# Gated linear attention on one core: the decay of a chunk in pairs of levels with shared keys, in blocks of 32 tokens

## The chip, the cores and the metric

The kernel runs on one core of a Trainium2 chip. The metric is the device time of one execution in microseconds (us); the time given for a kernel is the median of several runs. The profile is that of one further execution.

## What is computed

Two residual layers over 512 tokens of width 1024: a sparse attention layer and a layer of gated linear attention (GLA), each followed by a squared-ReLU MLP. The change lies in the GLA mixer. It has 4 heads with keys of 128 and values of 256. Its reference, in chunks of tokens, cut to what matters:

```python
def step(state, inp):
    qi, ki, vi, gi = inp
    b = jnp.cumsum(gi, axis=2)
    diff = jnp.where(mask, b[:, :, :, None, :] - b[:, :, None, :, :], -jnp.inf)
    attn = jnp.einsum('bhid,bhjd,bhijd->bhij', qi, ki, jnp.exp(diff))
    intra = jnp.einsum('bhij,bhje->bhie', attn, vi)
    inter = jnp.einsum('bhid,bhde->bhie', qi * jnp.exp(b), state)
    ...
```

The part that matters is `attn`: for each pair of a query i and an earlier key j of the same chunk, the sum over the 128 key dimensions d of q[i,d] k[j,d] exp(b[i,d] - b[j,d]), where b is the running sum of log gates. The exponent depends on i, j and d, so it is no plain matrix product.

## The kernel before, in words

The kernel takes 512 tokens as 4 chunks of 128. Large products (the projections and the MLP) are done in three float32r matmuls on a high and a low part of each operand (`mm3`, lines 186 to 188); these are called main products below. Weights come in by SyncE's DMA queue as `raw`; ScalarE makes the high part (line 130) and VectorE the low part (line 131). PSUM tiles of the pool `qk` have two buffers.

In `gla`, `qT`, `kT` and `bT` (trace: gq, gk, gb) hold queries, keys and running gate sums with the key dimension on partitions, heads and tokens along the row. `AT[c]` is the transposed `attn` of chunk c: 128 keys on partitions, 4 heads x 128 queries. It is made level by level (`LEVELS` 64, 32, 16, 8, 4, 2, 1). At level H the chunk is cut in blocks of 2H tokens. For a query in the right half and a key in the left half of a block, the exponent is split at the left half's last token m: exp(b[i]-b[m]) on the query and exp(b[m]-b[j]) on the key. Each pair i > j lies in just one level; the pairs i = j are the diagonal (li = -1), plain q times k.

`prepare(c, li)` makes the factors of a level in a tile E (5 buffers): two subtractions of 256 columns on GpSimd (923, 924), one exponential of 512 on ScalarE (925), and two products with keys and queries on VectorE (926, 927). `apply(c, li)` multiplies: for levels 64 and 32 in tiles of 64 or 32 columns, written by ScalarE into AT (944, 945); for levels 16 to 1 in one whole 128 x 128 product per head (948), most of whose result is of no use, from which VectorE copies what a mask admits into AT (949, 128 x 512). The diagonal is a whole product too (935), times the identity (936).

`work` lists the 32 steps (c, li). `around(n, tile_work)` emits the preparation of the next n steps, then a tile of main products of a panel, then the application of these steps: 2 per tile in the first value panel (346 columns), 3 in the second and in the first gate panel (512 columns). The tile framework's scheduler then sets the order on each engine. In the last gate panel `chunk_in` and `chunk_out` finish the chunks: they multiply AT with the values (985), take the running state in (987), norm and gate, and update the state (1003). `constants` loads the masks during the MLP before.

Of the kernel before, what the change touches and what calls it, by code (L numbers as in the profile page):

```python
# [47 lines left out]
LEVELS = [64, 32, 16, 8, 4, 2, 1]  # L48
BLOCK = 32
N_MASKS = sum(h < BLOCK for h in LEVELS)  # L50
# [16 lines left out]
def _consts():  # L67
# [18 lines left out]
    cu = np.stack([((p // (2 * h)) == (f // (2 * h))) & (p % (2 * h) < h) & (f % (2 * h) >= h) for h in LEVELS if h < BLOCK], axis=1)  # L86
# [8 lines left out]
class Trunk:  # L95
# [752 lines left out]
    def gla(self, w3, ba, gn, masks):  # L848
# [3 lines left out]
        with tc.tile_pool(name="gla", bufs=1) as gp, tc.tile_pool(name="glt", bufs=2) as gt:  # L852
# [50 lines left out]
            AT = [gp.tile([P, B_H, P], F32, name=f"AT{c}") for c in range(NT)]  # L903

# [5 lines left out]

            work = [(c, li) for c in range(NT) for li in range(-1, len(LEVELS))]
            ready = {}

            def prepare(c, li):

                if li < 0:
                    return
                H, cs = LEVELS[li], slice(c * P, (c + 1) * P)
                b, q, k = bT[:, :, cs], qT[:, :, cs], kT[:, :, cs]
                E = gt.tile([P, B_H, P], F32, name="E", bufs=5)  # L920
                left, right = halves(b, 0, H), halves(b, 1, H)
                bm = left[:, :, :, H - 1:H].to_broadcast([P, B_H, P // (2 * H), H])
                nc.gpsimd.tensor_tensor(halves(E, 0, H), bm, left, op=OP.subtract)
                nc.gpsimd.tensor_tensor(halves(E, 1, H), right, bm, op=OP.subtract)
                nc.scalar.activation(E, E, AF.Exp, scale=IT)
                nc.vector.tensor_mul(halves(E, 0, H), halves(E, 0, H), halves(k, 0, H))
                nc.vector.tensor_mul(halves(E, 1, H), halves(E, 1, H), halves(q, 1, H))
                ready[c, li] = E

            def apply(c, li):  # L930
                cs = slice(c * P, (c + 1) * P)
                ps = self.qk.tile([P, 512], F32, name="qk").rearrange("p (h s) -> p h s", s=P)
                if li < 0:
                    for h in range(B_H):
                        nc.tensor.matmul(ps[:, h, :], kT[:, h, cs], qT[:, h, cs], start=True, stop=True)
                    nc.vector.tensor_tensor(AT[c], ps, self.ident[:, None, :].to_broadcast([P, B_H, P]), op=OP.mult)
                    return
                E = ready.pop((c, li))
                H = LEVELS[li]
                if H >= BLOCK:  # L940
                    for j in range(0, P, 2 * H):
                        left, right = slice(j, j + H), slice(j + H, j + 2 * H)
                        for h in range(B_H):
                            nc.tensor.matmul(ps[left, h, right], E[:, h, left], E[:, h, right], start=True, stop=True)
                        nc.scalar.copy(AT[c][left, :, right], ps[left, :, right])
                    return
                for h in range(B_H):
                    nc.tensor.matmul(ps[:, h, :], E[:, h, :], E[:, h, :], start=True, stop=True)  # L948
                nc.vector.copy_predicated(AT[c], masks[:, li - len(LEVELS) + N_MASKS, None, :].to_broadcast([P, B_H, P]), ps)

            def chunk_in(c):
# [3 lines left out]
                eb = gt.tile([P, B_H, P], F32, name="E", bufs=5)  # L955
# [16 lines left out]
            def chunk_out(c, last):  # L972
# [7 lines left out]
                for a in range(0, B_H, 2):  # L980
# [8 lines left out]
                    for j in range(2):  # L989
                        h = a + j  # L990
                        nc.scalar.activation(junk[:, :B_DV], o[:, j, :], AF.Square, accum_out=ss[:, h:h + 1])
# [178 lines left out]
```

## Time and profile before

| | |
|---|---|
| median of 3 runs | 1160.45 us (1160.43 to 1160.72) |
| the profiled execution's own time | 1162.37 us |
| its span, first to last instruction | 1160.6 us |
| mean granted TensorE clock | 0.996 |
| busy: TensorE, VectorE, ScalarE, GpSimd | 1144.4, 890.5, 556.9, 212.3 us |
| the steps of `work`, first to last product | about 648 to 731 us of the span |

The names of the profile: PE is TensorE (PEld its weight loads), DVE VectorE, ACT ScalarE, POOL GpSimd, SP SyncE, whose queue starts the DMAs. L948 is line 948 of the kernel. A matmul's record is longer than the time until the next one starts, since matmuls are pipelined; a busy share of PE therefore can't be read as work at full rate.

### The profile page before, as it was taken

The numbers are of one execution on the slowest core, as the hardware profiler recorded it, in microseconds if no ns is written. First come the engines' busy times: TensorE is split into PE (matmuls) and PEld (weight loads), VectorE is DVE, ScalarE is ACT, GpSimd is POOL, SyncE is SP. The second block draws the span as 40 slices with busy tenths as digits, with TensorE's granted clock in tenths as the row PEclk, the third lists the DMA queues.
The fourth block names the chain that finished last, engine by engine and source line by source line (L and its number), as shares of the span: only waits on it lengthen the run. The fifth ranks groups of instructions, "written<-read, shape, count | busy, mean of one in ns | idle before, by whom it ended". The sixth has DMA issues, their size and how long they took to land. (4 is left out here: it accounts for less than half of the span.)

```text
span 1160.6 us, 15685 instructions
## 1 busy us (share of the span) xinstructions
PE 1144.4 (99%) x5847; PEld 963.0 (83%) x5847; DVE 890.5 (77%) x1587; ACT 556.9 (48%) x953; POOL 212.3 (18%) x144
## 2 busy tenths in 40 slices
PE   8999999999999999999999999999999999999997
PEld 7877888888888888888888998888988888888875
DVE  6799997687886786687864577766697866886787
ACT  6665786544444353344355444343453534444342
POOL 0000000002213203212302254110032032213221
PEclk9999999999999999999999999999999999999998
DMA  7322130521431441242241231233223422431421
GB/s 245 100 73 73 37 110 1 160 87 37 145 106 42 143 140 62 90 145 86 74 133 50 64 112 35 70 109 110 74 60 122 145 70 76 145 107 46 138 73 73
DMA packets 58196, 109.35 MB, mean 94 GB/s; under 512 B 5204, under 2 KB 10712, under 8 KB 58120
## 3 DMA queue, kind: packets, MB, share of 16 engines
q1 hardware_dynamic: 56968, 104.16, 28.1%
q0 software_dynamic: 1152, 4.19, 1.3%
q8 instruction: 46, 0.75, 0.3%
q14 instruction: 30, 0.25, 0.1%
HBM read 106.24 MB, written 2.10 MB: 93 GB/s over the span
## 5 line engine op out<-in xcount | busy, mean ns | idle before, releaser
L131 DVE TENSOR_TENSOR w_lo<-raw,w_hi 128x1024 fp32r<-128x1024 f32 (+4 forms) x220 | 289.3, 1333 | 27.5 <-ACT w_hi L130 25.1
L130 ACT CAST w_hi<-raw 128x1024 fp32r<-128x1024 f32 (+4 forms) x220 | 223.4, 1024 | 121.4 <-PE ps L188 43.8
L186 PE MATMUL ps<-XT,w_hi 128*128 128x512 f32 (+1 forms) x640 | 236.1, 369 | 0.0
L187 PE MATMUL ps<-XT,w_hi 128*128 128x512 f32 (+1 forms) x640 | 235.7, 368 | 0.0
L188 PE MATMUL ps<-XT,w_lo 128*128 128x512 f32 (+1 forms) x640 | 235.6, 368 | 0.0
L186 PE MATMUL ps<-w_hi,XT 128*128 128x512 f32 (+5 forms) x440 | 164.5, 374 | 0.8 <-ACT w_hi L130 0.8
L187 PE MATMUL ps<-w_lo,XT 128*128 128x512 f32 (+5 forms) x440 | 161.8, 368 | 1.1 <-DVE w_lo L131 1.1
L188 PE MATMUL ps<-w_hi,XT 128*128 128x512 f32 (+5 forms) x440 | 161.6, 368 | 0.0
L186 PEld LDWEIGHTS ps<-XT,w_hi 128*128 128x128 f32 x640 | 120.7, 189 | 20.2 <-issue 0.2
L187 PEld LDWEIGHTS ps<-XT,w_hi 128*128 128x128 f32 x640 | 120.7, 189 | 20.2 <-issue 0.4
L188 PEld LDWEIGHTS ps<-XT,w_lo 128*128 128x128 f32 x640 | 120.7, 189 | 20.1 <-issue 0.2
L152 POOL TENSOR_TENSOR raw<-raw 128x1024 f32<-128x1024 f32 x14 | 34.2, 2440 | 385.4 <-DVE w_lo L131 385.4
L186 PE MATMUL ps<-w_hi,form 128*128 128x512 f32 x260 | 102.3, 393 | 0.7 <-DVE big L408 0.7
L187 PE MATMUL ps<-w_lo,form 128*128 128x512 f32 x260 | 101.5, 390 | 0.0
L188 PE MATMUL ps<-w_hi,form 128*128 128x512 f32 x260 | 101.4, 390 | 0.0
L187 PEld LDWEIGHTS ps<-w_lo,XT 128*128 128x128 f32 x440 | 83.5, 190 | 11.9 <-DVE w_lo L131 1.7
L186 PEld LDWEIGHTS ps<-w_hi,XT 128*128 128x128 f32 x440 | 83.5, 190 | 11.5 <-ACT w_hi L130 1.0
L188 PEld LDWEIGHTS ps<-w_hi,XT 128*128 128x128 f32 x440 | 83.5, 190 | 10.8
L131 DVE TENSOR_TENSOR w_lo<-t,w_hi 128x1024 fp32r<-128x1024 f32 x14 | 30.4, 2168 | 72.7 <-ACT w_hi L130 72.7
L360 DVE TENSOR_TENSOR h<-h 128x512 f32<-128x512 f32 (+1 forms) x72 | 43.7, 624 | 44.1 <-ACT h L359 44.1
L359 ACT ACTIVATE h<-ps 128x512 f32<-128x512 f32 (+1 forms) x72 | 38.7, 546 | 61.7 <-PE ps L188 54.7
L130 ACT CAST w_hi<-t 128x1024 fp32r<-128x1024 f32 x14 | 14.7, 1051 | 105.2 <-POOL t L154 105.2
(238 smaller groups left out, 1986.1 us busy)
## 6 DMA issues: line engine op xcount, KB each, us to landing
raw<-in_mlp_w_up_dram SPq DMA_DIRECT2D x64, 512.0 KB, 4.5
raw<-in_mlp_w_down_dram SPq DMA_DIRECT2D x64, 512.0 KB, 4.6
raw<-in_b_w_in_dram SPq DMA_DIRECT2D x16, 512.0 KB, 4.6
raw<-in_a_w_in_dram SPq DMA_DIRECT2D x12, 512.0 KB, 4.3
big<-in_x_dram SPq DMA_DIRECT2D x8, 512.0 KB, 4.1
raw<-in_a_w_o_dram SPq DMA_DIRECT2D x8, 512.0 KB, 4.0
raw<-in_b_w_o_dram SPq DMA_DIRECT2D x8, 512.0 KB, 5.0
raw<-in_b_w_in_dram SPq DMA_DIRECT2D x8, 346.0 KB, 4.3
```

What stands on the lines that cost most here:

```text
L130: self.nc.scalar.copy(hi, src)
L131: self.nc.vector.tensor_sub(lo, src, hi.bitcast(F32))
L152: sub(t1, b12, b11)
L186: mmul(out, lhs[0], rhs[0], start=first, stop=False, skip_group_check=more)
L187: mmul(out, lhs[0], rhs[1], start=False, stop=False, skip_group_check=more)
L188: mmul(out, lhs[1], rhs[0], start=False, stop=last, skip_group_check=more)
L359: nc.scalar.activation(h, ps[:, :step], AF.Relu)
L360: nc.vector.tensor_mul(h, h, h)
```

## The change

The levels 16 to 1 and the diagonal, six steps per chunk, become three: `None` (level 1 and the diagonal), (2, 4) and (8, 16). Such a step works in blocks of 32 tokens, and its pairs i > j lie within one block of 32, so its product is done per head and block: 4 products per head of 32 keys by 48 columns, each written to its own strip of 32 partitions of a PSUM tile.

For a pair (H, G) with G = 2H, the keys are scaled once, to the last token of their own run of H tokens (one subtraction and exponential of 512 columns, one product with all keys). A tile Q (2 buffers) holds three kinds of queries, 64 per head each: of the right halves at level H; of the right halves at level G, for keys of the nearer run; and these times the decay over one run, for keys of the farther one. The step `None` uses plain keys, and Q holds all queries (put in an order of even and odd by ScalarE) and the odd ones with their decay.

The results of a chunk gather in a tile `near`, 128 keys by 4 x 32 queries. VectorE multiplies the diagonal's part with a small identity `eye` into it and copies 16 columns per head through a mask, once for level 1 and three times for each pair. After the step (2, 4), ScalarE puts the four blocks of 32 x 32 per head to their places in AT, which GpSimd clears ahead of all steps. Levels 64 and 32 are done as before. E has 3 buffers instead of 5. `work` has 20 steps, whose levels 64 and 32 stand among the others; the tiles of the panels take 1, 2 and 2 steps. The table of masks shrinks from 640 to 144 columns. The gate's tanh is written to its final place without a tile of its own.

```diff
+            work = [(c, level) for c in range(NT) for level in WIDE]
+            for i in range(2 * NT):
+                work.insert(NT + 2 * i, (i // 2, (64, 32)[i % 2]))
+            def exps(E, *parts):
+                for e, x, y in parts:
...
+                    nc.gpsimd.tensor_tensor(e, x, y, op=OP.subtract)
+                nc.scalar.activation(E, E, AF.Exp, scale=IT)
+            def queries(c, level):
...
+                Q = gt.tile([P, B_H, 192], F32, name="Q")
...
+                exps(Q[:, :, :P], (e[0], halves(b, 1, H), near[:, :, :, H - 1:H]),
+                     (e[1], halves(b, 1, G), far[:, :, :, G - 1:G]))
+                nc.vector.tensor_mul(e[1], e[1], halves(q, 1, G))
...
+                nc.vector.tensor_mul(e[2], e[1], over.to_broadcast(list(e[2].shape)))
+                nc.vector.tensor_mul(e[0], e[0], halves(q, 1, H))
...
-                E = gt.tile([P, B_H, P], F32, name="E", bufs=5)
+                E = gt.tile([P, B_H, P], F32, name="E", bufs=3)
+                if isinstance(level, tuple):
+                    bs, es = (x.rearrange("p h (n s) -> p h n s", s=level[0]) for x in (b, E))
+                    exps(E, (es, bs[:, :, :, level[0] - 1:level[0]], bs))
+                    nc.vector.tensor_mul(E, E, k)
...
-                for h in range(B_H):
-                    nc.tensor.matmul(ps[:, h, :], E[:, h, :], E[:, h, :], start=True, stop=True)
-                nc.vector.copy_predicated(AT[c], masks[:, li - len(LEVELS) + N_MASKS, None, :].to_broadcast([P, B_H, P]), ps)
...
                 for h in range(B_H):
+                    for j in range(0, P, BLOCK):
+                        own = Q[:, h, :].rearrange("p (a m) -> p a m", a=3)[:, :, j // 2:(j + BLOCK) // 2]
+                        nc.tensor.matmul(ps[j:j + BLOCK, h, :48].rearrange("p (a m) -> p a m", a=3),
+                                         K[:, h, j:j + BLOCK], own, start=True, stop=True)
...
+                for s, m, o in parts:
+                    mk = masks[:, None, m * 16:(m + 1) * 16].to_broadcast([P, B_H, 16])
+                    nc.vector.copy_predicated(halves(near[c], 1, s), mk.rearrange("p h (n s) -> p h n s", s=s),
+                                              ps[:, :, o:o + 16].rearrange("p h (n s) -> p h n s", s=s))
+                if level == WIDE[-1]:
+                    for j in range(0, P, BLOCK):
+                        own = slice(j, j + BLOCK)
+                        nc.scalar.copy(AT[c][own, :, own], near[c][own])
...
-            for c0, steps in ((332, 2), (678, 3)):
+            for c0, steps in ((332, 1), (678, 2)):
...
-                    around(3, gate_tile)
+                    around(2, gate_tile)
```

The order on the engines. Outside the GLA mixer it is the same but for the line numbers. On TensorE, a place at which tiles of level 32 stand, in the value panels; before:

```order
L188 MATMUL ps<-w_hi,XT 128x346
L944 MATMUL qk<-E 32x32 x4
L948 MATMUL qk<-E 128x128 x2
L944 MATMUL qk<-E 32x32 x4
L948 MATMUL qk<-E 128x128 x2
L186 MATMUL ps<-w_hi,XT 128x346
```

And such a place of the change (L197 to L199 are the main products, L990 levels 64 and 32, L997 the small products):

```order
L199 MATMUL ps<-w_hi,XT 128x346
L990 MATMUL qk<-E 32x32 x4
L997 MATMUL qk<-Q,E 32x48 x12
L990 MATMUL qk<-E 32x32 x4
L997 MATMUL qk<-Q,E 32x48 x4
L197 MATMUL ps<-w_hi,XT 128x346
```

Between the two halves of level 32 twelve small products now stand, in other places 14 or 15, where two whole ones stood.

On TensorE, the place where the last gate panel begins; before:

```order
L188 MATMUL ps<-w_hi,XT 128x512
L948 MATMUL qk<-E 128x128 x8
L968 MATMUL tps<-cft,E 128x128 x4
L186 MATMUL ps<-w_hi,XT 128x512
L187 MATMUL ps<-w_lo,XT 128x512
L948 MATMUL qk<-E 128x128 x4
L188 MATMUL ps<-w_hi,XT 128x512
```

And of the change (L1034 are the transposes of the line 968 before):

```order
L199 MATMUL ps<-w_hi,XT 128x512
L990 MATMUL qk<-E 32x32 x4
L997 MATMUL qk<-Q,E 32x48 x15
L990 MATMUL qk<-E 32x32 x4
L997 MATMUL qk<-Q,E 32x48
L1034 MATMUL tps<-cft,E 128x128 x4
L197 MATMUL ps<-w_hi,XT 128x512
```

The last step's products no longer stand among the last panel's main products.

On GpSimd, the beginning of the stage in the change; L453 and L447 of the MLP before (here L464, L458) were followed by the subtractions at once:

```order
L464 TENSOR_TENSOR big<-big 128x512 x3
L916 MEMSET AT_6178 128x512
L916 MEMSET AT_6179 128x512
L916 MEMSET AT_6180 128x512
L916 MEMSET AT_6181 128x512
L935 TENSOR_TENSOR Q<-gb 128x4x64
L935 TENSOR_TENSOR E<-gb 128x512 x2
L935 TENSOR_TENSOR E<-gb 128x4x64 x2
L935 TENSOR_TENSOR Q<-gb 128x4x64 x5
```

Four clearings stand ahead of the first subtraction, and whole subtractions of 512 columns stand among the halves.

## Rows read from the trace of the kernel before

**Rows 1.** The page's first part: busy time of each engine.

```profile
PE 1144.4 (99%) x5847; PEld 963.0 (83%) x5847; DVE 890.5 (77%) x1587; ACT 556.9 (48%) x953; POOL 212.3 (18%) x144
```

**Rows 2.** Windows: stretch, its length, busy us by engine, granted clock, DMA share, GB/s.

```profile
648.00:728.00 80.00, 78.87 (x554) 71.60 (x553) 56.50 (x88) 36.76 (x64) 37.26 (x50) 1.00 0.21 69
```

**Rows 3.** Groups by line and shape, 620 to 740 us: busy, mean ns | idle before.

```profile
L948 PE MATMUL qk<-E 128*128 128x128 f32 x160 | 21.3, 280 | 1.0 <-DVE AT L949 1.0
L935 PE MATMUL qk<-gq,gk 128*128 128x128 f32 x32 | 4.3, 278 | 0.0
L944 PE MATMUL qk<-E 128*32 128x32 f32 x64 | 3.5, 199 | 0.2 <-ACT AT L945 0.2
L944 PE MATMUL qk<-E 128*64 128x64 f32 x32 | 2.7, 228 | 0.0
```

**Rows 4.** Timeline of PE from 659.5: start us, length us, merged records.

```profile
659.50 0.32 PE L188 MATMUL ps<-w_hi,XT 128*128 128x346 f32 x1
659.66 1.95 PE L948 MATMUL qk<-E 128*128 128x128 f32 x16
```

**Rows 5.** Timeline of PE at 654.13, within a run of 32-column tiles.

```profile
653.95 0.35 PE L944 MATMUL qk<-E 128*32 128x32 f32 x6
```

**Rows 6.** Timeline of PE at 649.60, within a run of 64-column tiles.

```profile
649.43 0.34 PE L944 MATMUL qk<-E 128*64 128x64 f32 x3
```

**Rows 7.** Timeline of PE from 120.9, in the attention layer.

```profile
120.93 1.05 PE L724 MATMUL po<-vn,pT 128*128 128x65 f32 x8
```

**Rows 8.** Timeline of PE from 672.8, in and out of 32-column tiles.

```profile
672.90 0.32 PE L188 MATMUL ps<-w_hi,XT 128*128 128x346 f32 x1
673.15 0.44 PE L944 MATMUL qk<-E 128*32 128x32 f32 x8
673.52 0.43 PE L186 MATMUL ps<-w_hi,XT 128*128 128x346 f32 x1
673.79 0.32 PE L187 MATMUL ps<-w_lo,XT 128*128 128x346 f32 x1
```

**Rows 9.** Timeline of PE from 690.9; eight 64-column and eight 32-column records, merged.

```profile
691.00 0.32 PE L188 MATMUL ps<-w_hi,XT 128*128 128x346 f32 x1
691.25 1.05 PE L944 MATMUL qk<-E 128*64 128x64 f32 x16
692.22 0.50 PE L186 MATMUL ps<-w_hi,XT 128*128 128x512 f32 x1
```

**Rows 10.** Timeline of PE from 726.3, around the last whole products.

```profile
726.51 0.39 PE L187 MATMUL ps<-w_lo,XT 128*128 128x512 f32 x1
727.88 1.13 PE L948 MATMUL qk<-E 128*128 128x128 f32 x8 [0.97 <-DVE AT L949]
...
729.07 0.39 PE L186 MATMUL ps<-w_hi,XT 128*128 128x512 f32 x1
729.30 0.39 PE L187 MATMUL ps<-w_lo,XT 128*128 128x512 f32 x1
```

**Rows 11.** Groups of the other engines, 620 to 740 us.

```profile
L923 POOL TENSOR_TENSOR E<-gb 128x256 f32<-128x256 f32 x28 | 21.8, 779 | 111.9 <-DVE gb L891 62.7 <-PE qk L944 20.3 <-ACT big L1030 14.3
L924 POOL TENSOR_TENSOR E<-gb 128x256 f32<-128x256 f32 x28 | 20.3, 726 | 0.0
L925 ACT ACTIVATE E<-E 128x512 f32<-128x512 f32 x28 | 17.7, 632 | 30.8 <-POOL E L924 30.8
L949 DVE COPY_PREDICATED AT<-masks,qk 128x512 f32<-128x512 uint8 x20 | 14.7, 734 | 9.3 <-PE qk L948 5.9 <-ACT AT L945 3.4
L1042 POOL TENSOR_TENSOR gate<-gate,gn 128x512 f32<-128x512 f32 x5 | 6.6, 1320 | 14.2 <-DVE gate L1040 14.2
L936 DVE TENSOR_TENSOR AT<-qk,cft 128x512 f32<-128x512 f32 x4 | 2.7, 680 | 1.6 <-PE qk L935 1.6
L945 ACT COPY AT<-qk 32x128 f32<-32x128 f32 x8 | 2.0, 251 | 2.1 <-PE qk L944 2.1
```

More of the change, by code (lines that the diff above doesn't have):

```diff
@@ L47 @@
 TAU = 16.0
-LEVELS = [64, 32, 16, 8, 4, 2, 1]
+WIDE = (None, (8, 16), (2, 4))
 BLOCK = 32
-N_MASKS = sum(h < BLOCK for h in LEVELS)
+N_MASKS = 7
 NEG_MASKED = -3.0e38
@@ L85, in _consts, with mask @@
     cf = np.concatenate([a.astype(np.float32) for _, a in parts], axis=1)
-    cu = np.stack([((p // (2 * h)) == (f // (2 * h))) & (p % (2 * h) < h) & (f % (2 * h) >= h) for h in LEVELS if h < BLOCK], axis=1)
+    k, q = p % BLOCK, f[:, :BLOCK]
+    def mask(size, keys, half):
+        r = q[:, q[0] % size >= half]
+        return (k // size == r // size) & (k % size >= keys[0]) & (k % size < keys[1])
+    cu = [mask(2, (0, 1), 1)]
+    for h in (8, 2):
+        cu += [mask(2 * h, (0, h), h), mask(4 * h, (h, 2 * h), 2 * h), mask(4 * h, (0, h), 2 * h)]
+    cu = np.concatenate(cu + [k == q[:, 0::2], k == q[:, 1::2]], axis=1)
     return np.ascontiguousarray(cf), np.ascontiguousarray(cu.reshape(P, -1).astype(np.float32))
@@ L903, in gla @@
             AT = [gp.tile([P, B_H, P], F32, name=f"AT{c}") for c in range(NT)]
+            for a in AT:
+                nc.gpsimd.memset(a, 0.0)
             def halves(x, i, s):
                 return x.rearrange("p h (n two s) -> p h n two s", two=2, s=s)[:, :, :, i, :]
[L911 to L916, printed above, removed]
-                    return
-                H, cs = LEVELS[li], slice(c * P, (c + 1) * P)
-                b, q, k = bT[:, :, cs], qT[:, :, cs], kT[:, :, cs]
-                E = gt.tile([P, B_H, P], F32, name="E", bufs=5)
[L921 to L928, printed above, removed]
@@ L943, in apply @@
+            def apply(c, level):
+                K, Q = ready.pop((c, level))
+                if level in (64, 32):
+                    ps = self.qk.tile([P, 512], F32, name="qk").rearrange("p (h s) -> p h s", s=P)
+                    for j in range(0, P, 2 * level):
+                        left, right = slice(j, j + level), slice(j + level, j + 2 * level)
                         for h in range(B_H):
-                            nc.tensor.matmul(ps[left, h, right], E[:, h, left], E[:, h, right], start=True, stop=True)
+                            nc.tensor.matmul(ps[left, h, right], K[:, h, left], Q[:, h, right], start=True, stop=True)
@@ new lines, in apply @@
+                if level is None:
+                    near[c] = gt.tile([P, B_H, BLOCK], F32, name="near")
+                    nc.vector.tensor_tensor(near[c].rearrange("p h (m two) -> p h two m", two=2),
+                                            ps[:, :, :BLOCK].rearrange("p h (two m) -> p h two m", two=2),
+                                            eye[:, None, :, :].to_broadcast([P, B_H, 2, 16]), op=OP.mult)
+                    parts = [(1, 0, 32)]
+                else:
+                    m = 1 + 3 * (level == (2, 4))
+                    parts = [(level[0], m, 0), (level[1], m + 1, 16), (level[1], m + 2, 32)]
```

71 lines of the change are left out of this document (46 added, 25 removed).

## The prediction

> **What bounds the kernel now.** I read the busy shares first, then the stage by windows, then the groups of instructions, then the timeline of TensorE. PE is busy over 99% of the span [rows 1], which by itself says little, since records of a pipelined engine overlap. The stage that the change touches, from 648 to 728 us, shows the same: PE 78.9 of 80 us, DVE 56.5, ACT 36.8, POOL 37.3, at a granted clock of 1.00 (the 2.4 GHz level) [rows 2]. So what counts there is the spacing of PE's records and the few places at which PE waits; the other engines lie beside it. An fp32 matmul of the program leaves two records, so the 24 matmuls of a chunk at levels 16 to 1 and on the diagonal are 48 records, 192 over four chunks; the groups list 160 and 32 of them [rows 3].
>
> The spacing of records in a run is read from a merged row: its length, less the duration of one record, over the count less one. For 128 columns loaded and 128 streamed: (1.95 - 0.28)/15 = 0.111 us [rows 3, 4]. For tiles of 32 columns with 32 streamed: (0.35 - 0.199)/5 = 0.030 us inside a run [rows 3, 5], or (0.44 - 0.199)/7 = 0.034 us with the slower first step of a run [rows 3, 8]. For 64 and 64: (0.34 - 0.228)/2 = 0.056 us [rows 3, 6]. A row of the attention has 128 columns loaded and 65 streamed, and its records of about 0.275 us stand (1.05 - 0.275)/7 = 0.111 us apart [rows 7]: the larger of the two widths sets the spacing, at about 0.9 ns per column.
>
> **What PE loses.** The 96 whole products, 192 records x 0.111 = **21.3 us**, all on the path.
>
> **What PE gains.** Three steps for each of four chunks, each with 16 matmuls of 32 columns loaded and 48 streamed: 192 matmuls, 384 records. No row shows this shape. In width it lies between 0.030 (32) and 0.056 (64), which are 11.5 and 21.5 us; if nothing overlaps, half way between them, 0.043, or 16.5 us. What is new besides is that each matmul goes to the next strip of 32 output partitions, where the 32-wide tiles of before stay in one strip through a run. I take 0.034, the whole run of eight 32-column records [rows 8]: the weight load is the same, and of the 16 more columns streamed I expect that they lie beside the neighbour strip's load. 384 x 0.034 = **13.1 us**.
>
> **Going into and out of tiles.** From the main product at 672.90 to the second one after the tiles at 673.79 it is 0.89 us [rows 8]; two main products at 0.16 and eight records at 0.030 make 0.56, so an excursion costs 0.33: 0.09 before the first tile, 0.13 before the next main product starts, the rest behind it. The run with both tile sizes takes 1.22 us from 691.00 to 692.22 [rows 9]; less one main product, 8 x 0.056 and 8 x 0.030, and the 0.09 and 0.13, 0.15 is left for the change between the sizes. Before there are 11 excursions and 1 such change; in the changed order I count 12 and 4. That adds 0.33 + 3 x 0.15 = **0.8 us**.
>
> **PE's waits.** Before, PE loses 1.14 us at 726.51 (1.37 to the next record, less the 0.23 of one main product of 512 columns) ahead of a product that needs the buffer of the one before [rows 10], and 0.2 ahead of a second half of level 32 [rows 3]: 1.3 together. In the changed order all steps stand ahead of the last gate panel, so the first goes. The second half of level 32 still waits for ScalarE's copy of the first (0.25 us [rows 11]); 12 to 15 small products now stand between, 0.8 to 1.0 us. For new waits on the two qk buffers I charge half of what goes: **-0.7 us**, with 0 and -1.3 as ends.
>
> **Beside PE.** DVE sheds 20 masked copies of 0.734 and 4 diagonal products of 0.680, 17.4 us [rows 11], and gets 28 copies of 64 elements and 4 products of 128. Pro rata these are 3.2 us, at the price of the old ones 23.3; I estimate 0.25 each, 8 us, nearer the lower end, as an eighth of the elements is copied. Its products are 56 halves before, and now 40 halves and 8 whole ones, worth 56: even. ACT sheds 4 of 28 exponentials at 0.632 for half ones, and gets 4 query copies (taken as 0.63) and 16 placements of 32 partitions at 0.25: about +6 us on 36.8 of 80. POOL's 56 half subtractions, at 0.779 and 0.726 42 us, become 36 halves and 8 whole ones at 1.32 (the row of the same size), 38 us, plus 4 clearings of AT, under 1.32 each. Those stand ahead of its first subtraction, before which it waited 62.7 us [rows 11]. All of this fits beside PE and costs nothing; where that cover fails is the third rival. The smaller table, cast and mask load lie in the MLP before and change no wait of PE. SP's order is the same.
>
> **The sum.** -21.3 + 13.1 + 0.8 - 0.7 = -8.1 us. The execution profiled took 1162.37 us with a span of 1160.6; the sum makes it 1154.3. The median of the three runs stands 1.9 lower, at 1160.45, so the forecast is **1152.3 us**. After this stage PE stays busy up to the end, so what is saved is not given back.
>
> A rule of the Trainium skill speaks against the change. Row first: 32-column records stand 0.030 us apart and 64-column ones 0.056 [rows 5, 6], so the narrow ones pay half, and the trace does not bear the rule out. The Trainium skill, "TensorEngine Tiling (Array Packing)", section "Instruction Overhead", has it that a matmul pays some 60 cycles whatever it streams, and that one column is as slow as 60. By that, 48 columns would cost what 60 do.
>
> **Rivals.**
>
> *Serial strips.* Strips do not overlap at all and the larger width sets the spacing: 0.043 x 384 = 16.5, sum -4.7, **1155.8 us**. For it: every row above follows the larger width. Against: none of them changes strip inside a run. It gets 0.31.
>
> *Sixty columns.* The narrow records cost what 60 columns would, 60 x 0.9 = 0.053: 20.4 us, sum -0.8, **1159.7 us**, no change. The rows of 32 columns are against it. 0.03. (This is the rule just named.)
>
> *Strips side by side.* All four strips load and stream at once: 0.043/4 = 0.011, 4.1 us, sum -17.1, **1143.4 us**. No row shows fewer than 0.030 between any two records of this kind, and the two records of one matmul share a strip, so they can't overlap. 0.05. The Trainium skill's "TensorEngine Tiling (Array Packing)", section "Key Properties", says that tiles work independently and load and multiply in parallel; no run so far shows it here.
>
> *A wait in place of the products.* Key and query buffers: E has 3 instead of 5, Q 2, so POOL can prepare less far ahead. In a value tile with two steps it has one whole and four half subtractions, 1.32 + 4 x 0.75 = 4.3 us [rows 11]; PE has 24 x 0.16 + 32 x 0.034 + 8 x 0.030 + 0.33 + 0.15 = 5.6 us. It decides from 1.07 us per half on; at 1.5 us POOL is 1.7 us late in each of the four such tiles, and 6.9 us of the gain go: **1159.2 us**. The gate tiles stream 512 columns and have more cover. For it: POOL's halves vary where DVE works beside them (mean 0.779, where the other half has 0.726). Against: a whole tile of slack in the first panel. 0.09.
>
> *Each change of strip drains PE* (the other side). The size changes show 0.09 us each on the way in [rows 8]. If going to another strip of the same size costs the same, all 192 matmuls pay: 17.3 us on the serial case, +12.6, **1173.1 us**. It decides from 0.024 us per change on (4.7/192), measured from the serial case. No row excludes it, as no run of tiles in this trace changes strip. 0.08. By the Trainium skill, "TensorEngine Tiling (Array Packing)", section "Key Properties", it is a change of mode, and not of the tile alone, that drains the engine; the rows show the drain at changes of size and say nothing on the other.
>
> **How the numbers follow.** The forecast, records from 0.030 to 0.038 apart (1150.7 to 1153.9), has 0.44. The serial case has 0.31 and, with the ends of the waits, reaches 1155 to 1158. The range starts at 1147.5: two strips side by side, 0.022, give 8.3 us and -12.9. It ends at 1158.0. Left out are the four strips (0.05), the drain (0.08) and most of the late buffers and the sixty columns (some 0.08). A measurement of this kernel can tell 0.2%, 2.3 us: under 1158.1 is faster, over 1162.8 slower. Faster: 0.44 + 0.05 + 0.30 of the serial case = 0.79. Same: 0.01 of the serial case, 0.03 of the sixty columns, 0.07 of the late buffers = 0.11. Slower: the drain with 0.08 and 0.02 of the late buffers = 0.10.
>
> **What would show it.** In the group of the small products: 384 records, and the merged rows of 32 of them about 1.3 us long; 1.55 and more is the serial case, under 0.9 side by side, 3 or more the drain. The group of masked copies on DVE should be under 0.4 us each, and its idle time should grow. Ahead of the small products PE should show under 1 us of idle time in all; several us there, ended by DVE or by ACT's exponentials, would be the late buffers. Main products must keep their spacing of 0.16 and 0.23 us [rows 4, 10]. The forecast is wrong if the stage's gain on PE is under 6 or over 11 us, or if a gain there comes back as idle time of PE later.

## The result and the profile after

Four runs of the change give a median of **1145.52 us** (1145.34 to 1149.05), four of the kernel before 1160.59 (1160.43 to 1162.27): a ratio of **0.9874, 95% interval 0.9853 to 0.9895**. The gain is 15.1 us where 8.1 were forecast, and the time lies 2 us under the range. Runs of one kernel differ by 2 to 4 us, so where single times are compared below, they are those of its fastest runs: about 1160.2 for before, 1145.4 for the change. TensorE's clock has a part in this: in the profiled execution of before the granted clock is 0.83 from 20 to 30 us, which is 3.4 of the 10 us at half (1.2 GHz); in that of the change it is 1.00 there and through the stage.

The stage runs from the first small product to the first product of the chunks' output. The PE timelines of the kernel before and of the change show these two places (start us, length us, then the record):

```profile
648.28 1.06 PE L935 MATMUL qk<-gq,gk 128*128 128x128 f32 x8
...
733.86 1.02 PE L985 MATMUL po<-big,AT 128*128 128x256 f32 x4
```

```profile
646.06 0.55 PE L997 MATMUL qk<-Q,gk 128*32 128x48 f32 x32
...
716.42 1.02 PE L1051 MATMUL po<-big,AT 128*128 128x256 f32 x4
```

85.58 us have become 70.36: **15.2 us are gained inside this stage** and nowhere else. (The later start of before is its early stretch at half clock: in the profile of the change run again, below, which has such a stretch too, the first small product starts at 648.25.) From the stage's end to the end of the span it is 426.7 us before and 427.2 now, so 0.5 us are given back there.

The page's first part and the window of 648 to 728 us of the change, to be read beside [rows 1, 2]:

```profile
PE 1126.0 (98%) x6039; PEld 943.5 (82%) x6039; DVE 883.2 (77%) x1592; ACT 563.7 (49%) x973; POOL 212.9 (19%) x136
```

```profile
648.00:728.00 80.00, 76.77 (x788) 66.00 (x787) 60.07 (x121) 49.30 (x100) 37.41 (x41) 1.00 0.25 80
```

PE still bounds the kernel, but a window of the same 80 us now has 3.2 us in which PE does nothing (1.1 before), and ACT is busy 49.3 us instead of 36.8. (The window reaches 12 us into the chunks' output now, so the shares of the other engines are not those of the stage alone.)

The groups of the change, 610 to 740 us, which answer to [rows 3, 11] (busy us, mean ns | idle before, by what it ended):

```profile
L997 PE MATMUL qk<-Q,E 128*32 128x48 f32 x256 | 5.3, 209 | 0.0
L997 PE MATMUL qk<-Q,gk 128*32 128x48 f32 x128 | 2.5, 209 | 0.0
L990 PE MATMUL qk<-E 128*32 128x32 f32 x64 | 3.5, 199 | 2.7 <-ACT AT L991 2.5
L1010 DVE COPY_PREDICATED near<-masks,qk 128x64 f32<-128x64 uint8 x28 | 6.8, 244 | 3.5 <-PE qk L997 3.1
L1015 ACT COPY AT<-near 32x128 f32<-32x128 f32 x16 | 4.7, 295 | 2.3 <-DVE near L1010 2.1
L945 ACT COPY Q<-gq 128x512 f32<-128x512 f32 x4 | 4.6, 1142 | 0.1
```

384 small records are there, as counted, with no idle time ahead of them. The masked copies take 0.244 us each (0.25 was estimated). The idle time ahead of level 32's 32-column records has grown from 0.2 to 2.7 us.

How long the small products take is in the PE timeline of the change:

```profile
650.31 0.31 PE L199 MATMUL ps<-w_hi,XT 128*128 128x346 f32 x1
650.55 0.55 PE L997 MATMUL qk<-Q,E 128*32 128x48 f32 x32
651.03 0.42 PE L197 MATMUL ps<-w_hi,XT 128*128 128x346 f32 x1
651.29 0.32 PE L198 MATMUL ps<-w_lo,XT 128*128 128x346 f32 x1
```

A merged row of 32 records is 0.55 us long, where the forecast had about 1.3: (0.55 - 0.209)/31 = **0.011 us per record**. The unmerged records of the same trace say how. Start us, duration ns, tile:

```
650.618   206 PE L997 MATMUL qk<-Q,E 128*32 128x48 f32
650.625   206 PE L997 MATMUL qk<-Q,E 128*32 128x48 f32
650.632   206 PE L997 MATMUL qk<-Q,E 128*32 128x48 f32
650.638   206 PE L997 MATMUL qk<-Q,E 128*32 128x48 f32
650.661   206 PE L997 MATMUL qk<-Q,E 128*32 128x48 f32
650.668   206 PE L997 MATMUL qk<-Q,E 128*32 128x48 f32
650.674   206 PE L997 MATMUL qk<-Q,E 128*32 128x48 f32
650.681   206 PE L997 MATMUL qk<-Q,E 128*32 128x48 f32
```

Four records start 0.007 us apart, read here as one for each strip (a record does not name its strip; the first experiment tests the reading); then it takes until 0.043 after the first of them before each strip gets its next record. So the strips run side by side, and 0.043 is what one strip needs, the price that the forecast had worked out for 48 columns if nothing overlaps.

The new wait is in the timelines of PE and ACT of the change:

```profile
682.42 0.34 PE L990 MATMUL qk<-E 128*32 128x32 f32 x5 [2.13 <-ACT AT L991]
```

```profile
678.95 2.92 ACT L141 CAST w_hi<-raw 128x1024 fp32r<-128x1024 f32 x3
681.78 0.43 ACT L1096 COPY big<-ps 128x346 f32<-128x346 f32 x1
682.12 0.25 ACT L991 COPY AT<-qk 32x128 f32<-32x128 f32 x1
```

The second half of level 32 waits for ScalarE's copy of the first half, and ScalarE has three weight casts of some 1 us and a value copy ahead of that copy. The list of waits for PE's weight loads, 646 to 763 us (us in total, times, longest), puts the whole at:

```profile
PEld qk L990 <- ACT AT L991: 3.2, 4, 2.3
...
PEld qk L1069 <- ACT S L1071: 0.9, 1, 0.9
```

### The profile page after: what moved, and what is told of

Same layout as the page of the kernel before. It is cut to its first block, busy times and chain, and to the rows that moved or that the text cites. A ratio compares the mean times of both kernels' runs of the same rounds, so it can differ in the third digit from the quotient of the medians.

```text
span 1143.6 us, 16057 instructions
## 1 busy us (share of the span) xinstructions
PE 1126.0 (98%) x6039; PEld 943.5 (82%) x6039; DVE 883.2 (77%) x1592; ACT 563.7 (49%) x973; POOL 212.9 (19%) x136
## 5 line engine op out<-in xcount | busy, mean ns | idle before, releaser
L197 PE MATMUL ps<-XT,w_hi 128*128 128x512 f32 (+1 forms) x640 | 236.0, 369 | 0.0
L199 PE MATMUL ps<-XT,w_lo 128*128 128x512 f32 (+1 forms) x640 | 235.5, 368 | 0.0
L197 PE MATMUL ps<-w_hi,XT 128*128 128x512 f32 (+5 forms) x440 | 163.7, 372 | 0.8 <-ACT w_hi L141 0.8
L199 PE MATMUL ps<-w_hi,XT 128*128 128x512 f32 (+5 forms) x440 | 160.3, 365 | 0.0
L197 PEld LDWEIGHTS ps<-XT,w_hi 128*128 128x128 f32 x640 | 120.6, 189 | 20.2 <-issue 0.2
L199 PEld LDWEIGHTS ps<-XT,w_lo 128*128 128x128 f32 x640 | 120.6, 188 | 20.1 <-issue 0.2
L197 PE MATMUL ps<-w_hi,form 128*128 128x512 f32 x260 | 102.2, 393 | 0.7 <-DVE big L419 0.7
L199 PE MATMUL ps<-w_hi,form 128*128 128x512 f32 x260 | 101.4, 390 | 0.0
L197 PEld LDWEIGHTS ps<-w_hi,XT 128*128 128x128 f32 x440 | 82.8, 188 | 12.0 <-ACT w_hi L141 1.0
L199 PEld LDWEIGHTS ps<-w_hi,XT 128*128 128x128 f32 x440 | 82.8, 188 | 10.9
L141 ACT CAST w_hi<-t 128x1024 fp32r<-128x1024 f32 x14 | 14.7, 1049 | 105.3 <-POOL t L165 105.3
```

The costliest lines, as they stand in the source:

```text
L141: self.nc.scalar.copy(hi, src)
L197: mmul(out, lhs[0], rhs[0], start=first, stop=False, skip_group_check=more)
L199: mmul(out, lhs[1], rhs[0], start=False, stop=last, skip_group_check=more)
```

## The experiments

Times are medians; the kernel before was run beside each batch, and its fastest runs took 1159.9 to 1160.7 each time.

**The same strip four times in a row.** All four heads of a block, then the next block:

```diff
-                for h in range(B_H):
-                    for j in range(0, P, BLOCK):
+                for j in range(0, P, BLOCK):
+                    for h in range(B_H):
```

> The change, but the small products go strip by strip: for each block of 32 tokens the four heads one after the other, so four matmuls (eight records) in a row stay in one strip. Same work, same sizes. Theory (strips run side by side because neighbouring matmuls of the program lie in different strips): the spacing goes from 0.011 us per record to the serial 0.043 of the 48 columns, 384 x 0.032 = 12.3 us more, about 1157.8 us against 1145.5 of the change. Rival (TensorE looks far enough ahead to find the other strips, or a narrow tile is cheap by its area whatever its neighbour is): spacing stays at 0.011 to 0.02 and the time within 1145 to 1149 us.

1151.16 us (1149.29 to 1151.27), ratio 0.9913 [0.9898, 0.9927]; its fastest run, 1149.29, takes 3.9 more than the change. The same 384 records, in the timeline and the groups of this kernel:

```profile
653.33 1.13 PE L997 MATMUL qk<-Q,E 128*32 128x48 f32 x32
```

```profile
L997 PE MATMUL qk<-Q,E 128*32 128x48 f32 x256 | 9.5, 209 | 0.0
```

(1.13 - 0.209)/31 = 0.030 us each. Single records of one strip stand 0.043 apart (653.440, 653.482, 653.525), and the next strip begins at 653.531, when three records of the old one are still to come: the eight records of a strip advance the run by 0.20 us, not by 8 x 0.043 = 0.34. So neighbours in one strip are serial and neighbours in different strips are not, and TensorE reached no more than three records ahead here. Both expectations missed: 0.030 lies between the serial 0.043 and the 0.011 of the rival. The products cost 12 x 0.58 = 7.0 us more; 3 us of that don't reach the end, since the longer products cover level 32's wait (0.7 us of it is left, from 3.2).

**Two strips of 64** instead of four of 32:

```diff
-                    for j in range(0, P, BLOCK):
+                    for j in range(0, P, 64):
...
-                        nc.tensor.matmul(ps[j:j + BLOCK, h, :48].rearrange("p (a m) -> p a m", a=3),
-                                         K[:, h, j:j + BLOCK], own, start=True, stop=True)
+                        nc.tensor.matmul(ps[j:j + 64, h, :96].rearrange("p (a m) -> p a m", a=3),
+                                         K[:, h, j:j + 64], own, start=True, stop=True)
```

> The change, but the small products go in two strips of 64 tokens (64 keys by 96 columns) per head instead of four of 32 (32 by 48). The masked copies still take the first 16 columns of each kind, so half of the blocks are filled from columns that belong to others. 192 records instead of 384, each as wide as 96 columns. Theory (all strips side by side): 0.086 / 2 = 0.043 us per record, 8.3 us instead of 4.2, so 4 us more than the change, about 1149.6. Rival (only neighbours of the narrowest kind overlap, or the narrow tiles are cheap for another reason): 0.086 per record, 16.5 us, about 1157.8.

1148.57 us in one run, with the clock at 1.00 as in the profile of the change, 3.2 more than the change. In its timeline:

```profile
650.88 0.88 PE L997 MATMUL qk<-Q,E 128*64 128x96 f32 x16
```

(0.88 - 0.253)/15 = 0.042 us, with 0.253 the mean of its group. At 0.9 ns per column 96 columns alone are 0.086: two strips halve the price, four quarter it. The theory holds.

**No strips, all else as in the change.** One whole product of 128 keys and 128 query columns per head and step:

```diff
-                    for j in range(0, P, BLOCK):
...
+                    nc.tensor.matmul(ps[:, h, :], K[:, h, :], Q[:, h, :P], start=True, stop=True)
```

> The change without the strips: per head one product of all 128 keys with the first 128 of the 192 query columns instead of four of 32 keys with 48. The third kind of queries is left out of the product, and the masked copies take the same columns for all blocks. 96 records at 0.111 us, 10.7 us, instead of 384 at 0.011, 4.2 us. Theory (strips and shorter copies each carry a part): 6.5 us more on TensorE, less what the waits ahead of level 32 then hide (up to 3): 1149 to 1152 us. Rival (the three steps instead of six and the compact tile make the whole gain, the strips none): within 1.5 us of the change, 1144 to 1147.

1149.11 us (1148.84 to 1149.34), ratio 0.9890 [0.9875, 0.9904]. In its timeline:

```profile
650.70 1.05 PE L995 MATMUL qk<-Q,E 128*128 128x128 f32 x8
```

These 96 records at (1.05 - 0.290)/7 = 0.109 are 10.5 us, half of the 21.3 before, and **11 of the 15 us are there without a single strip**, at the lower end of what the theory had. (The third kind of queries stays out of the product here, so AT lacks its part, and the run only serves to price the strips.) The strips bring 3.7 on top, of the 6.3 that their records save: most of the rest is lost to the wait of level 32, of which the list has 3.2 us in the change and the timeline here one of 1.12.

**Strips alone.** The kernel before with strips at levels 16 to 1, and nothing paired; each block's result goes to its place by a masked copy of its own:

```diff
-                    nc.tensor.matmul(ps[:, h, :], E[:, h, :], E[:, h, :], start=True, stop=True)
-                nc.vector.copy_predicated(AT[c], masks[:, li - len(LEVELS) + N_MASKS, None, :].to_broadcast([P, B_H, P]), ps)
+                    for own in blocks:
+                        nc.tensor.matmul(ps[own, h, own], E[:, h, own], E[:, h, own], start=True, stop=True)
+                for own in blocks:
+                    mk = masks[own, li - len(LEVELS) + N_MASKS, None, own].to_broadcast([BLOCK, B_H, BLOCK])
+                    nc.vector.copy_predicated(AT[c][own, :, own], mk, ps[own, :, own])
```

> The kernel before, with one part of the change alone: at levels 16 to 1 each whole product of 128 x 128 becomes four of 32 x 32 in the four strips, and four masked copies per step take their results. All seven levels, the diagonal as a whole product, five E buffers and the order of work stay. Theory (the strips make the gain): 160 records at 0.111, 17.8 us, become 640 at 0.008 to 0.011, 5 to 7 us: a gain of 11 to 13 us, about 1148 to 1149.5. Rival (taking levels in pairs, with fewer steps and shorter copies, makes the gain): under 5 us gained, 1155 or more.

1159.66 us (1159.05 to 1161.84, ten runs), ratio 0.9991 [0.9981, 1.0000]: about 1 us, with an interval that reaches none. Groups, timeline and windows of this kernel:

```profile
L953 DVE COPY_PREDICATED AT<-masks,qk 32x128 f32<-32x128 uint8 x80 | 23.9, 299 | 7.4 <-PE qk L950 5.2
L950 PE MATMUL qk<-E 128*32 128x32 f32 x640 | 8.9, 199 | 1.2 <-DVE AT L953 1.2
```

```profile
657.17 0.76 PE L950 MATMUL qk<-E 128*32 128x32 f32 x64
...
667.80 1.13 PE L935 MATMUL qk<-gq,gk 128*128 128x128 f32 x8 [1.06 <-DVE AT L953]
...
672.84 0.44 PE L944 MATMUL qk<-E 128*32 128x32 f32 x8 [2.40 <-DVE AT L936]
```

```profile
646.00:726.00 80.00, 74.35 (x1049) 63.05 (x1048) 60.88 (x143) 35.77 (x62) 38.06 (x50) 0.98 0.25 78
...
675.00:678.00 3.00, 3.00 (x12) 3.00 (x13) 0.76 (x2) 0.80 (x2) 1.19 (x2) 0.57 0.02 5
```

The products became as cheap as expected: (0.76 - 0.199)/63 = 0.009 us, 640 x 0.009 = 5.7 us for the 17.8 of 160 records. Yet 80 masked copies of 0.299 take the place of 20 of 0.734 [rows 11], 9.2 us more on VectorE; PE then waits on VectorE for buffers (1.06, 2.40 us), and after the long wait its granted clock falls to 0.57 over 675 to 678 us; 3.4 us at half cost 1.7. The stage is still 3.3 us shorter than before (82.3 us), but 2.1 are given back in the chunks' output, most of them in one more wait for VectorE, in the same timeline:

```profile
734.34 0.65 PE L972 MATMUL tps<-cft,E 128*128 128x128 f32 x4 [1.45 <-DVE E L969]
```

The theory's prices came out, its gain did not. The rival's time did (1155 or more): faster products alone only moved the bound to VectorE. The Trainium skill, "TensorEngine Tiling (Array Packing)", section "PSUM Bottleneck", warns that after a fourfold speed-up of TensorE the copies out of PSUM may become the bottleneck; this run shows it.

**Strips alone, with more PSUM buffers** (the products of levels 16 to 1 in the transposes' pool):

```diff
-                ps = self.qk.tile([P, 512], F32, name="qk").rearrange("p (h s) -> p h s", s=P)
+                if li < 0 or LEVELS[li] >= BLOCK:
+                    ps = self.qk.tile([P, 512], F32, name="qk").rearrange("p (h s) -> p h s", s=P)
+                else:
+                    ps = self.tp.tile([P, 4, P], F32, name="tps")
```

> The kernel before with strips alone (1159.7 us, where TensorE waited for VectorE's copies out of the two qk buffers, and lost more to a stretch at the half clock), and levels 16 to 1 write to the two transpose buffers, so four PSUM buffers are in use. Theory (strips alone lose their gain because the copies to AT hold the buffers): with more buffers 3 us or more come back, 1156.5 us or less. Rival (the copies themselves, 80 at 0.3 us, bound the stage, so more buffers only move the wait): within 1.5 us of 1159.7.

1160.64 us (1158.82 to 1162.57, ten runs), ratio 0.9993 [0.9984, 1.0003]: nothing. In its timeline the longest wait only grew:

```profile
672.88 0.64 PE L947 MATMUL qk<-E 128*32 128x32 f32 x8 [3.51 <-DVE AT L939]
```

The clock is at half for 6.8 us here, from 672.2 on, against 3.4 with strips alone, which costs 1.7 more; set aside, the stage is some 0.8 us shorter than with strips alone, not 3. So it is VectorE's work that is late, as the rival had it, far more than the number of buffers.

**Strips and compact tile, but no pairs.** The kernel before with strips, the compact tile and ScalarE's placing, level by level:

```diff
-                nc.vector.copy_predicated(AT[c], masks[:, li - len(LEVELS) + N_MASKS, None, :].to_broadcast([P, B_H, P]), ps)
+                    for own in blocks:
+                        nc.tensor.matmul(ps[own, h, :BLOCK], E[:, h, own], E[:, h, own], start=True, stop=True)
+                nc.vector.copy_predicated(near[c], masks[:, li - len(LEVELS) + N_MASKS, None, :].to_broadcast([P, B_H, BLOCK]), ps[:, :, :BLOCK])
+                if li == len(LEVELS) - 1:
+                    for own in blocks:
+                        nc.scalar.copy(AT[c][own, :, own], near[c][own])
```

> The kernel before with strips and the compact tile, but without taking levels in pairs: six steps per chunk at levels 16 to 1 and the diagonal, each 16 products of 32 x 32 in four strips, one masked copy of 128 elements into the compact tile (24 copies instead of 80 of the kernel with strips alone), four placements by ScalarE per chunk, 5 key and query buffers. Theory (the compact tile's short copies are what lets the strips' gain through, the pairs add little): 192 records at 0.111, 21.3 us, become 768 at about 0.009, 6.9 us, and VectorE gets under what it had before: 10 to 14 us gained, about 1146.5 to 1150. Rival (half as many steps, that is the pairs, are needed, as GpSimd's and VectorE's preparation of 28 steps now bounds the stage): TensorE waits for preparation, under 6 us gained, 1154 or more.

(Here the diagonal goes in strips too, and the gate's tanh is written in place, as in the change.)

1157.02 us (1156.80 to 1159.09, six runs), ratio 0.9972 [0.9959, 0.9984]. But this kernel was late before the stage began: its first small product starts at 649.58 us without the early drop of the clock, 3.5 later than in the change, and its products on `form` in the layers before take 392 to 399 ns instead of 389. Its constants are shorter, which moves what stands behind them in SBUF; in the change the padding behind `reset` had been lengthened to 180 columns. Two runs put that to the test, and the change itself was run once more beside the kernel without pairs.

> The change itself, beside the kernel without pairs on the same chip. Every theory: 1145.3 to 1147.6 us.

1146.54 us (1145.51 to 1149.32), ratio 0.9881 [0.9863, 0.9899], as in its first runs. Its products on `form` take 389 ns on this chip too, so the chip is not what the kernel without pairs paid. The profile is that of its slowest run, 1149.32 us. A window of it:

```profile
646.00:730.00 84.00, 80.77 (x830) 69.43 (x829) 61.83 (x127) 49.75 (x100) 38.32 (x42) 0.98 0.28 90
```

Its list of waits in the stage is that of the first profile, but here the clock falls to half from 685.9 to 689.3 us, after the 2.1 us of waiting for level 32, and the stage takes 71.96 us instead of 70.36. So that wait can cost another 1.6 us, and does not always.

**The same without pairs, with 88 more columns of padding**, and **the change with 88 fewer**:

```diff
-            T.reset = gc.tile([P, SEQ + 88], F32, name="reset")[:, :SEQ]
+            T.reset = gc.tile([P, SEQ + 176], F32, name="reset")[:, :SEQ]
```

```diff
-            T.reset = gc.tile([P, SEQ + 180], F32, name="reset")[:, :SEQ]
+            T.reset = gc.tile([P, SEQ + 92], F32, name="reset")[:, :SEQ]
```

> Levels one at a time with strips, compact tile and ScalarE's placing, as in the run without pairs, but the padding behind the constant `reset` is 88 columns (352 bytes a partition) longer, so that the constants take as much of SBUF as in the kernel before. In the run without pairs the large products that read `form`, long before the stage, took 392 to 399 ns instead of 389, and the stage began 3.4 us late; by itself the stage was 7.2 us shorter than before. Theory: the shorter constants moved the address of `form`, and that is what these products paid; with the padding they take 389 ns again, the stage begins at about 646.1, and the time is about 1153.5 us (1160.2 less some 7). Rival: the 3.4 us come from something else (the chip, the execution); then the products stay at 392 to 399 ns and the time at 1157.

> The change as it is, with the padding behind `reset` 88 columns (352 bytes a partition) shorter, and nothing else. Theory (the address of the operands counts): the products on `form` rise from 389 to between 392 and 399 ns, the stage begins 3 to 4 us later, and the time is about 1149 us at the lower level; the stage itself stays at 70.4 us. Rival (it was not the address): 1145.4 us, as the change.

With the padding, the kernel without pairs takes 1153.34 us (1152.19 to 1155.37), ratio 0.9946 [0.9929, 0.9964]; the change without it 1150.46 (1149.07 to 1152.82), ratio 0.9918 [0.9902, 0.9934]. The operations on `form`, 300 to 600 us, of the first and of the second (records, then ns least/median/most, first and last start):

```profile
L189 PE MATMUL ps<-w_hi,form x119: 389/389/481, 299.7 to 579.3; 128*128 128x512 f32 x119
```

```profile
L199 PE MATMUL ps<-w_hi,form x121: 388/399/477, 300.2 to 584.5; 128*128 128x512 f32 x121
```

Both went as the theory of the address had it; by the fastest runs it is 4.6 us less for the one and 3.7 more for the other. But the 4.6 are not the address alone. The window of 640 to 700 us without the padding and with it:

```profile
640.00:700.00 60.00, 56.24 (x859) 50.50 (x858) 37.56 (x68) 30.30 (x57) 29.01 (x37) 0.97 0.32 101
```

```profile
640.00:700.00 60.00, 56.24 (x866) 50.23 (x865) 41.48 (x74) 30.82 (x58) 33.18 (x41) 1.00 0.32 101
```

Without the padding the clock was at half from 674.1 to 677.6 us, after a wait of 2.2 us, and the stage took 78.40 us; with it the same wait left the clock alone, and it took 76.86. The address shows in the starts of the stage: 649.58 against 646.63 without pairs, and 651.84 against 648.25 for the change, each time in two profiles with the same early clock. So 352 bytes of padding decide over 3.0 and 3.6 us, in products that the edit doesn't name; which property of the address counts, and of which operand, was not tried. What the kernel without pairs is worth is then 1152.2 against 1160.2, between its theory (10 to 14 us) and the rival (under 6): **8 us for strips and compact tile, 7 more for the pairs**. In the timeline and groups of the padded kernel:

```profile
669.58 0.44 PE L952 MATMUL qk<-E 128*32 128x32 f32 x8 [2.21 <-DVE near L944]
```

```profile
L958 DVE COPY_PREDICATED near<-masks,qk 128x128 f32<-128x128 uint8 x20 | 6.0, 300 | 5.7 <-PE qk L957 5.3
```

The masked copies cost 6.0 us instead of 14.7 [rows 11] and 23.9 with strips alone; with them most of the strips' gain comes through. Two smaller things have a part in the 7 us between strips alone and this kernel: the clock, which fell there and not here (1.7 us), and the diagonal in strips, by the prices above 32 x 0.111 less 128 x 0.009, some 2.4 us. The wait behind VectorE is still there; in the change, with half the steps, the list shows none on VectorE. Whether it is the number of steps or the work in each was not tried.

**Level 32's copies after all its products**, and its two halves in turn, which takes the new wait apart:

```diff
-                    for j in range(0, P, 2 * level):
-                        left, right = slice(j, j + level), slice(j + level, j + 2 * level)
-                        for h in range(B_H):
+                    parts = [(slice(j, j + level), slice(j + level, j + 2 * level)) for j in range(0, P, 2 * level)]
+                    for h in range(B_H):
+                        for left, right in parts:
                             nc.tensor.matmul(ps[left, h, right], K[:, h, left], Q[:, h, right], start=True, stop=True)
+                    for left, right in parts:
                         nc.scalar.copy(AT[c][left, :, right], ps[left, :, right])
```

> The change, but in levels 64 and 32 all matmuls of a step are issued first, the two halves of level 32 in turn, and ScalarE's copies to AT follow; so the second half no longer waits for the copy of the first, which in the profile of the change stands behind three weight casts once. Theory: the idle time ahead of the second halves (2.3, 0.5, 0.3 and 0.25 us, 3.3 together) goes, about 1142 us. Rival: the copies are late anyway and the next user of the qk buffers waits for them instead, so the time stays within 1 us of 1145.5.

1143.72 us (1143.62 to 1145.76), ratio 0.9858 [0.9842, 0.9875]: 1.7 less than the change, half of the 3.2 that the wait was, and between the two expectations. PE's waits in this kernel:

```profile
PE qk L998 <- DVE near L1011: 1.7, 1, 1.7
PE qk L1070 <- ACT S L1072: 1.3, 1, 1.3
```

By the gaps between PE's records the 3.3 us of waiting for level 32 are gone. The edit does a second thing that its theory left out: the two halves, now in turn, lie in two strips, and sixteen of their records start within 0.25 us, where eight took 0.24; that is some 0.9 us over four steps. Against these stand two other waits, 1.7 us on VectorE's masked copies and 0.8 more than in the change in the chunks' output: 3.3 + 0.9 - 1.7 - 0.8 = 1.7.

**The same, with the small products in the transposes' PSUM pool**, and then **also every second state update there**:

```diff
-                ps = self.qk.tile([P, 512], F32, name="qk")[:, :B_H * 64].rearrange("p (h s) -> p h s", s=64)
+                ps = self.tp.tile([P, 4, P], F32, name="tps").rearrange("p a s -> p (a s)")[:, :B_H * 64].rearrange("p (h s) -> p h s", s=64)
```

```diff
-                        ds = self.qk.tile([P, 512], F32, name="qk").rearrange("p (h e) -> p h e", e=B_DV)
+                        if a == 0:
+                            ds = self.qk.tile([P, 512], F32, name="qk")
+                        else:
+                            ds = self.tp.tile([P, 4, P], F32, name="tps").rearrange("p a s -> p (a s)")
+                        ds = ds.rearrange("p (h e) -> p h e", e=B_DV)
```

> The kernel with the copies last (1143.7 us), and the small products write to the two PSUM buffers of the transposes, which are free in this stage, so levels 64 and 32 keep the two qk buffers for themselves. Theory: the 1.9 us that the small product then waited for a buffer that VectorE's masked copies still read, behind a weight subtraction, goes: about 1141.8 us. Rival: the copies are the late thing whatever the buffers, so the wait moves on to the next step or to the end of the stage: within 0.7 us of 1143.7.

> As the kernel with own PSUM buffers for the small products, and in the last gate panel the second pair of heads of the state update writes to a transpose buffer as well, so that its first product doesn't wait for ScalarE's copy of the first pair (0.8 us in the change, 1.6 with the copies last). Theory: 1 to 1.6 us less than without this step, about 1140.5 us. Rival: the transposes then wait for the same buffer, and nothing or up to 1 us is lost.

The first takes 1144.89 us (1143.72 to 1145.67), ratio 0.9856 [0.9839, 0.9872], and its fastest run, 1143.72, the same as without, as the rival had it; the second **1142.02** (1141.57 to 1144.31), ratio **0.9833 [0.9818, 0.9847]**, 3.6 less than the change by the fastest runs and the fastest kernel here. The one wait left in the second's list for the stage and the chunks' output:

```profile
PE tps L998 <- DVE E L973: 1.5, 1, 1.5
```

It is as long as in the run before it and nearly as long as with the old buffers (1.7, ended there by a masked copy, here by the key product): VectorE is late at this place, whichever buffer the result goes to. The wait in the chunks' output was one of buffers, and went, with a gain of some 2 us where 1 to 1.6 were expected.

## Why the prediction was wrong

**What PE loses** was right: 96 whole products left, and the price of 0.111 us per record fits the whole products of the run without strips (0.109).

**What PE gains** is the step that failed. It put 384 records at 0.034 us, 13.1 us; they stand 0.011 apart, 4.2 us. Two sentences led there. "In width it lies between 0.030 and 0.056" took rows from runs that stay in one strip as bounds for runs that don't; and of strips side by side it said that "the two records of one matmul share a strip, so they can't overlap". The premise is true, as 0.043 us between the records of one strip shows, but nothing follows from it: while one strip works through its two records the other three work on theirs. That rival had the right price (0.011), and its 1143.4 us is 2 us from the result; with 0.05 it was given far too little, since the argument against it rested on rows that could not show it. The Trainium skill's "TensorEngine Tiling (Array Packing)", section "Key Properties", has tiles load and multiply in parallel; the trace agrees (0.011 us against 0.043), and the order of the loops decides whether it comes to that (0.030 with one strip four times in a row).

**Going into and out of tiles** was right: 0.24 us from the start of the last main product to the first small one, and 0.26 from the first main product after them to the second, in the rows of 650.31 to 651.29, against 0.25 and 0.27 in [rows 8].

**PE's waits** had the wrong sign. The wait of 1.14 us at the last gate panel [rows 10] went, as said. But "12 to 15 small products now stand between, 0.8 to 1.0 us" was worked out with the price that failed: three times quicker, they cover 0.3 us or so. And the 0.25 us of ScalarE's copy left out that ScalarE may have other work ahead of it: three casts, for 2.3 us in one place. By the gaps between its records PE waits 3.3 us for level 32 over the stage, where before it waited some 1.7 in all (1.1 of them at the last gate panel); the term was +1.6 us, not -0.7.

With the measured terms the sum is -21.3 + 4.2 + 0.8 + 1.6 = -14.7 us, and the stage shows -15.2, of which 0.5 are given back in the chunks' output.

**Beside PE** was right in that nothing there cost time by itself. VectorE's masked copies are as estimated (0.244 us against 0.25). ScalarE's query copies are not: 1.142 us each against 0.63. They are the ones that put even and odd columns apart, but no run tells whether that is the reason. They add 2 us to an engine with room. That the smaller table costs nothing held because the padding behind `reset` keeps the addresses behind it; without the 352 bytes the change loses 3.6 us, which the prediction did not think of.

**The rivals.** Serial strips, the sixty columns and the drain at a change of strip all fall with the 0.007 us between records of different strips. The late buffers don't show: no idle time ahead of the small products. (No run gives the change more key or query buffers, so that rival was not tried by itself.) Among the signs, "under 0.9 side by side" is the one that came true.

One reading the prediction did not offer: the sum of PE's terms is not what each part of the change is worth. Strips alone bring 1 us, strips with the compact tile 8, pairs with the compact tile but without strips 11, all together 15.

## What to carry to other kernels

A price read from runs that never change a resource (here the strip) is no bound for runs that do; where the rows can't show an overlap, give it a chance by the mechanism and not by their silence. When products become several times quicker, work out anew every wait that they covered, with what the waited-for engine has queued ahead, and look whether the engine that empties PSUM keeps up: strips alone brought 1 us, until the copies shrank with them. When constants change size, keep the addresses behind them where they were, or compare with them kept.

## What the runs showed of the hardware that was not expected

Four 32-column strips of fp32 products run side by side: 0.007 us from strip to strip and 0.043 within one; two strips of 64 with 96 columns streamed give 0.042 per record. With one strip four times in a row only part of that is left, 0.030: the next strip begins when three of the eight records of the old one are still to come.

The address of an operand in SBUF, moved by 352 bytes, takes the large float32r products on `form` from 389 to between 392 and 399 ns, 3.0 us (without pairs) and 3.6 us (the change) up to the stage. That is seen as the edit's effect; the property of the address that counts is open.

The granted clock fell to 0.57 (half, 1.2 GHz, for most of the stretch) for 3 us after a wait of 2.40 us of PE in the stage with strips alone. After the same wait of one kernel it can fall or stay: in the change, with 2.1 us, it stayed at 1.00 in one profile and was at half for 3.4 us in another; without pairs, with 2.2 us, it was at half for 3.4 us without the padding and stayed at 1.00 with it. By the lengths of the stage that cost 1.6 and 1.5 us. What decides between the two was not settled.
